# A streaming encoder layer: the convolution's gated input computed with tokens on partitions

## The chip, the cores and the metric

The kernel runs on one core of a Trainium2 chip. A core has five engines that run side by side, each with its own queue of instructions: TensorE (matrix products and transposes, PE in the profile, its weight loads PEld), VectorE (DVE), ScalarE (ACT), GpSimd (POOL) and SyncE (SP, which here issues most of the transfers between main memory and the core). TensorE writes to eight PSUM tiles of 128 x 512 fp32, which VectorE and ScalarE read. The metric is the device time of one execution in microseconds (us); less is better.

## What is computed

One inference step of one layer for 384 tokens: 256 of a new stream and 8 x 16 of running streams. Cut to what matters here:

```python
h = rmsnorm(x, norm_mix_g)                      # x: 384 x 2048
proj = h @ w_in                                 # columns: GLU in | q | k | v | forget | gate A | gate B
u = glu_in[..., :D_CONV] * sigmoid(glu_in[..., D_CONV:])      # D_CONV = 1024
ext = concatenate([conv_buf, u], axis=1)
z = layernorm(causal_dwconv(ext, conv_dw_w, conv_dw_b), ...)  # 31 taps
a_out = (z * sigmoid(z)) @ conv_pw_out
new_conv = ext[:, -(CONV_W - 1):]               # an output
q = rmsnorm(q, q_norm_g); k = rmsnorm(k, k_norm_g)            # 8 heads of 128
b_out = attn_fn(q, k, v, logf) @ w_att_out
x = x + (gate_a * a_out + gate_b * b_out) @ w_out
# then a gated feed-forward with a 3-tap convolution
```

Outputs are x, the new keys, values and forget logarithms, and the convolutions' new states, all in fp32.

## The kernel before

**Tiling.** 384 tokens are three blocks of 128. The normed input is kept transposed, features on partitions (`hT`, four tiles of four 128-feature blocks). To keep fp32 accuracy every operand of a large product is split into a high and a low part (`hi`, `lo`), and each product is three matmuls: high by high, high by low, low by high (L239 to L241, L244 to L246).

**Weights.** `plan` is the list of all weight tiles in order. `ahead` fetches the next ones (two or three in advance; three raw and three split buffers) and `split` makes the high part on ScalarE (L145) and the low part on VectorE (L146). A pair of 128-row blocks of weights is one fetch, one split, and then the matmuls.

**Jobs.** `gemm` runs a list of jobs, each a block of columns of a projection. A job of kind "B" puts tokens on the output partitions: three PSUM tiles, up to 512 columns. A job of kind "A" puts features there: four PSUM tiles of 384 tokens. PSUM has five tiles in `acc` and three in `misc`; a job takes `acc` tiles, side work takes `misc`. When the last product of a job is done its `evac` functions read the tiles. After each k step `tick` lets side work take one step; TensorE runs everything in the order in which the program emits it.

**Stages around the change.** First stage: value blocks 0 and 1 run together, while `x_chunk` turns the input into `hT`, two blocks at a time, on TensorE (transposes L285, high part L288 on ScalarE, low part L289 on VectorE), and `first_norm` sums squares and gets the row scale `rs1`. Then value block 2, keys, queries. Then the gated input in four jobs of kind "A", with two side works: attention, one head every six steps (`head_operands` turns that head's queries and keys with six TensorE transposes, L583 and L587; `head_scores`, `head_probs`, `head_out`, `head_last`), and the convolution: `conv` lets channel block c start `CONV_LAG` steps after block c-1; its taps are VectorE instructions (L720, L722), and `fill` copies the block's input and turns its last rows on TensorE (L708, L709) to write the state. Next the two gates, beside the rest of the convolution and its LayerNorm (`layer_norm`, its first product is L779), the output projections, and the feed-forward.

**Order.** On ScalarE, VectorE and GpSimd a planner orders instructions by priority and by its own estimate of time; `tc.high_priority(offset=...)` moves a block ahead (`SPLIT_AHEAD` for splits, `EVAC_AHEAD` for evacuations). `queued` chains an instruction behind the newest chained one of its engine, so that the chain runs in the order of the program text. Before, only SP's first transfers are chained.

**Turning on VectorE.** A VectorE transpose works on blocks of 32 x 32. `blocks` (L255) turns a panel of 512 features with 16 such instructions, by writing each 32-row band to its place:

```python
for b in range(4):
    for a in range(4):
        nc.vector.transpose(put(a, slice(32 * b, 32 * b + 32)), src[32 * a:32 * a + 32, b])
```

It is used before the change for the mixed output, the second norm and the feed-forward.

Of the kernel before, what the change touches and what calls it, by code (L numbers as in the profile page):

```python
# [15 lines left out]
P = 128  # L16
# [3 lines left out]
H = 8  # L20
# [9 lines left out]
CONV_FIRST, CONV_LAG = 24, 17  # L30
# [3 lines left out]
SPLIT_AHEAD, EVAC_AHEAD = 150, 400  # L34
# [6 lines left out]
def hybrid_step(  # L41
# [66 lines left out]
    make_identity(nc, ident[:])  # L108

    def newton_rsqrt(r, s, m):  # L110
        nc.scalar.activation(s, m, AF.Sqrt)
# [32 lines left out]
    def split_rows(hi, lo, raw, o, k):  # L144
        nc.scalar.copy(hi[:, k, :o], raw[:, k, :o])  # L145
        tt(lo[:, k, :o], raw[:, k, :o], f(hi[:, k, :o]), op=ALU.subtract)  # L146
# [44 lines left out]
    v_last = len(plan) - 16  # L191
    ready = []
# [28 lines left out]
    def gemm(jobs, sides=()):  # L221
        for js in jobs:
            js = js if isinstance(js, tuple) else (js,)
            for j in js:
                nb = 4 if j["kind"] == "A" else NTT
                j["ps"] = [(misc_tile if j is not js[0] and i == 2 else acc_tile)() for i in range(nb)]
            for j, k in [(j, k + i) for k in range(0, js[0]["nk"], 2) for j in js for i in range(2)]:
# [7 lines left out]
                for m in range(nb):  # L235
                    s = slice(m * P, (m + 1) * P)
                    if j["kind"] == "A":
                        o = ps[m][:, :NT]
                        mm(o, hi[:, kk, s], ah, start=st, stop=False)  # L239
                        mm(o, hi[:, kk, s], al, start=False, stop=False)  # L240
                        mm(o, lo[:, kk, s], ah, start=False, stop=sp)  # L241
                    else:
                        o = ps[m][:, :n]
                        mm(o, ah[:, s], hi[:, kk, :n], start=st, stop=False)  # L244
                        mm(o, ah[:, s], lo[:, kk, :n], start=False, stop=False)  # L245
                        mm(o, al[:, s], hi[:, kk, :n], start=False, stop=sp)  # L246
                if sp:
                    with tc.high_priority(offset=EVAC_AHEAD):
                        for m in range(nb):
                            j["evac"](m, ps[m])  # L250
                    if "done" in j:
# [3 lines left out]
    def blocks(rows, put):  # L255
        src = rows.rearrange("p t (m b j) -> p b m t j", m=4, b=4)
# [11 lines left out]
    def job(kind, nk, act, evac, n=512, done=None):  # L268
        d = dict(kind=kind, nk=nk, act=act, evac=evac, n=n)
# [12 lines left out]
    def x_chunk(c):  # L282
# [5 lines left out]
        nc.scalar.activation(hi, ps[:, :NT], AF.Identity, scale=g)  # L288
        stt(lo, ps[:, :NT], g, f(hi), op0=ALU.mult, op1=ALU.subtract)  # L289
# [34 lines left out]
    rs1b = cp.tile([P, NT], F32, name="rs1b")  # L324
# [22 lines left out]
    for v, r, n in rows:  # L347
        nc.gpsimd.dma_start(vrow[r:r + n, :], v[0].rearrange("(c p) -> c p", p=P))
    kg = p_qkv.tile([P, P], F32, name="kg")
    nc.gpsimd.dma_start(kg[:], k_norm_g[0].partition_broadcast(P))  # L350
    bf = p_qkv.tile([P, H], F32, name="bf")
    nc.gpsimd.dma_start(bf[:], b_forget[0].partition_broadcast(P))
# [35 lines left out]
    def first_norm():  # L388
        for c in range(2, 16, 2):
# [6 lines left out]
            if c % 4 == 2:  # L396
                for t in range(NTT):
                    n = c // 4
                    tc.keep_in_program_order(
                        nc.scalar.activation(junk[:], xs[n][:, t, :], AF.Square, accum_out=ssx[:, t, n:n + 1]))  # L400
            yield
            if c > 2:
                yield
        mt = p_x0.tile([P, NTT], F32, name="mt")
        nc.vector.tensor_reduce(mt[:], ssx[:], axis=mybir.AxisListType.X, op=ALU.add)
        ts(mt[:], mt[:], 1.0 / DM, EPS, op0=ALU.mult, op1=ALU.add)
        r = rsqrt(mt[:], [P, NTT], p_x0, "r1")
        nc.vector.tensor_copy(rs1[:], r[:])
        for _ in range(12):
            yield  # L410
        small_columns()
        yield
        dg = diagonals(p_x0.tile([P, NTT, P], F32, name="r1d"), rs1)
        yield
        yield
        over_partitions(dg, rs1b[:])
# [6 lines left out]
    def tok_evac(dst, c0, n, sq=None, shared=True):  # L423
        def ev(t, ps):
            if shared and t % 2:
                ts(dst[:, t, c0:c0 + n], ps[:, :n], rs1[:, t:t + 1], None, op0=ALU.mult)
            else:
                nc.scalar.activation(dst[:, t, c0:c0 + n], ps[:, :n], AF.Identity, scale=rs1[:, t:t + 1])
            if sq is not None:
                for i in range(n // P):  # L430
                    jk = p_qkv.tile([P, P], F32, tag="jk", bufs=2, name="jk")
                    h = c0 // P + i
                    nc.scalar.activation(jk[:], dst[:, t, h * P:(h + 1) * P], AF.Square,
                                         accum_out=ssq[:, sq, t, h:h + 1])
# [3 lines left out]
    v_jobs = [job("B", 16, ha, tok_evac(vt, 344 * i, 344, shared=i == 2), n=344) for i in range(3)]  # L438
    gemm([(v_jobs[0], v_jobs[1]), v_jobs[2]], [first_norm()])
    close_x0()  # L440
# [23 lines left out]

    nc.sync.dma_start(prompt_v[0, 0].rearrange("(t p) h d -> p t (h d)", p=P), vt[:, 0:2, 0:1024])
    nc.sync.dma_start(sample_v[0].rearrange("b t h d -> (b t) (h d)"), vt[:, 2, 0:1024])
# [47 lines left out]
    gemm([job("B", 16, ha, tok_evac(kt, 512 * i, 512, 0)) for i in range(2)], [bias_rows()])  # L514
    close_b()
    rk = head_rsqrt(0)
# [6 lines left out]

    gemm([job("B", 16, ha, tok_evac(qt, 512 * i, 512, 1)) for i in range(2)])
# [548 lines left out]
```

## Time and profile before

| | |
|---|---|
| median of 3 runs | 2005.61 us (2002.94 to 2005.78) |
| the profiled execution | 2005.83 us |
| its span, first to last instruction | 2003.9 us |
| granted TensorE clock, mean | 0.999 |
| matmul records | 9431 |
| bytes moved | 275.99 MB, mean 138 GB/s |
| first stage with value blocks (first product 7.21, keys from 85.74) | 78.5 us |
| keys and queries (85.74 to 218.46) | 132.7 us |
| gated input and attention (218.46 to 390.05) | 171.6 us |

In the profile a group's row names the line, the engine, the operation, the tiles it writes and reads and how often it ran; then its busy time, the mean of one in ns, and the idle time before it with what ended it. A row of the timeline gives the start, the duration, the engine and the instruction, and in brackets the wait just before it. A row of windows gives the stretch, its length, then busy time and count for PE, PEld, DVE, ACT and POOL, the granted clock, the share of time in which the transfer engines were busy, and GB/s. Matmuls overlap: their pace is read from starts.

### The profile page before, as it was taken

The page shows a single profiled execution, that of the slowest core. Times are in us where ns is not written, and L with a number is a line of the kernel's source. Part 1 is how long each engine was busy: PE and PEld are TensorE (multiplying, and loading weights), DVE is VectorE, ACT ScalarE, POOL GpSimd, SP SyncE. Part 2 cuts the span into 40 slices and gives each one's busy share as a digit, 9 for nine tenths or more (in the row PEclk, how much of TensorE's full clock was granted, in tenths as well). Part 3 has the DMA queues.
Part 4 walks back from the last instruction along what each step waited for, and adds up shares of the span by engine and source line. Part 5 has one row for each costly group of instructions (what it writes and reads, how often), then busy time and mean ns, then how long its engine had stood idle before and what let it go on. Part 6 is the DMA issues. An engine that isn't in the chain of part 4 may idle for free.

```text
span 2003.9 us, 24493 instructions
## 1 busy us (share of the span) xinstructions
PE 1992.6 (99%) x9431; PEld 1681.5 (84%) x9431; DVE 1272.2 (63%) x1852; ACT 742.1 (37%) x1077; POOL 87.2 (4%) x216
## 2 busy tenths in 40 slices
PE   8999999999999999999999999999999999999999
PEld 8988999988888887888888888888888888888887
DVE  4435478888765487676867683367673376638663
ACT  5434455433334523334433432233332233323321
POOL 2000001100000000000010000001000000000000
PEclk9999999999999999999999999999999999999999
DMA  6566566444444334534444444444443444344443
GB/s 179 176 175 175 137 163 167 120 140 131 132 134 125 127 121 142 185 121 133 127 137 116 137 127 137 126 127 126 129 135 127 133 120 137 126 129 125 137 157 106
DMA packets 209254, 275.99 MB, mean 138 GB/s; under 512 B 55878, under 2 KB 96729, under 8 KB 209129
## 3 DMA queue, kind: packets, MB, share of 16 engines
q1 hardware_dynamic: 208817, 273.85, 46.3%
q8 instruction: 74, 1.21, 0.2%
q0 software_dynamic: 288, 0.57, 0.2%
q14 instruction: 43, 0.35, 0.1%
q10 hardware_dynamic: 32, 0.01, 0.0%
HBM read 266.98 MB, written 7.86 MB: 137 GB/s over the span
## 4 chain that ended last, share of the span: by engine, by line
PE 95%; DVE 4%; issue 1%; DMA 1%; ACT 0%; SPq 0%; ACTq 0%; DVEq 0%
PE acc L244 28%; PE acc L246 28%; PE acc L245 28%; PE acc L239 2%; PE acc L241 2%; PE acc L240 2%; DVE mixT L259 1%; DVE lo L146 1%; DMA raw<-in_w_in_dram 1%; DVE sgA L843 0%; DVE uT L259 0%; DVE sgA L844 0%; PE misc L636 0%; PE misc L603 0%; PE misc L285 0%
## 5 line engine op out<-in xcount | busy, mean ns | idle before, releaser
L146 DVE TENSOR_TENSOR lo<-raw,hi 128x1024 fp32r<-128x1024 f32 (+2 forms) x481 | 579.6, 1205 | 582.7 <-ACT hi L145 579.0
L145 ACT CAST hi<-raw 128x1024 fp32r<-128x1024 f32 (+2 forms) x481 | 496.0, 1032 | 994.2 <-PE acc L246 869.1
L244 PE MATMUL acc<-hi,xg 128*128 128x512 f32 x1056 | 411.8, 390 | 0.0
L246 PE MATMUL acc<-hi,xg 128*128 128x512 f32 x1056 | 410.9, 389 | 0.0
L245 PE MATMUL acc<-lo,xg 128*128 128x512 f32 x1056 | 410.8, 389 | 0.0
L244 PE MATMUL acc<-hi,hT 128*128 128x512 f32 (+1 forms) x704 | 268.5, 381 | 2.4 <-ACT hT L288 2.4
L246 PE MATMUL acc<-hi,hT 128*128 128x512 f32 (+1 forms) x704 | 266.0, 378 | 0.4 <-DVE hT L289 0.4
L245 PE MATMUL acc<-lo,hT 128*128 128x512 f32 (+1 forms) x704 | 265.8, 377 | 0.0
L244 PEld LDWEIGHTS acc<-hi,xg 128*128 128x128 f32 x1056 | 198.2, 188 | 42.3
L246 PEld LDWEIGHTS acc<-hi,xg 128*128 128x128 f32 x1056 | 198.2, 188 | 41.3
L245 PEld LDWEIGHTS acc<-lo,xg 128*128 128x128 f32 x1056 | 198.2, 188 | 40.6
L244 PE MATMUL acc<-hi,act 128*128 128x512 f32 x528 | 205.5, 389 | 0.5 <-DVE y L1018 0.5
L246 PE MATMUL acc<-hi,act 128*128 128x512 f32 x528 | 205.4, 389 | 0.0
L245 PE MATMUL acc<-lo,act 128*128 128x512 f32 x528 | 205.4, 389 | 0.0
L722 DVE SCALAR_TENSOR_TENSOR ut<-ext,cw,ut 128x384 f32<-128x384 f32 x240 | 151.5, 631 | 6.1
L244 PEld LDWEIGHTS acc<-hi,hT 128*128 128x128 f32 x704 | 132.7, 189 | 25.3 <-ACT hT L288 2.7
L246 PEld LDWEIGHTS acc<-hi,hT 128*128 128x128 f32 x704 | 132.7, 189 | 23.3 <-DVE hT L289 0.7
L245 PEld LDWEIGHTS acc<-lo,hT 128*128 128x128 f32 x704 | 132.8, 189 | 22.2
L259 DVE STREAM_TRANSPOSE extf<-tok 32x384 f32<-32x384 f32 x176 | 100.3, 570 | 30.9 <-ACT tok L954 28.2
L259 DVE STREAM_TRANSPOSE uT<-tok 32x384 f32<-32x384 f32 x176 | 100.3, 570 | 29.7 <-ACT tok L954 26.9
L244 PEld LDWEIGHTS acc<-hi,act 128*128 128x128 f32 x528 | 99.1, 188 | 21.6 <-DVE y L1018 0.9
L245 PEld LDWEIGHTS acc<-lo,act 128*128 128x128 f32 x528 | 99.1, 188 | 20.5
(289 smaller groups left out, 2079.7 us busy)
## 6 DMA issues: line engine op xcount, KB each, us to landing
raw<-in_w_up_dram SPq DMA_DIRECT2D x176, 512.0 KB
raw<-in_w_in_dram SPq DMA_DIRECT2D x96, 512.0 KB
raw<-in_w_down_dram SPq DMA_DIRECT2D x88, 512.0 KB
raw<-in_w_in_dram SPq DMA_DIRECT2D x64, 256.0 KB
raw<-in_w_out_dram SPq DMA_DIRECT2D x32, 512.0 KB
raw<-in_w_att_out_dram SPq DMA_DIRECT2D x16, 512.0 KB
raw<-in_conv_pw_out_dram SPq DMA_DIRECT2D x16, 512.0 KB
raw<-in_w_in_dram SPq DMA_DIRECT2D x23, 344.0 KB
```

The source lines that it names most:

```text
L145: nc.scalar.copy(hi[:, k, :o], raw[:, k, :o])
L146: tt(lo[:, k, :o], raw[:, k, :o], f(hi[:, k, :o]), op=ALU.subtract)
L239: mm(o, hi[:, kk, s], ah, start=st, stop=False)
L240: mm(o, hi[:, kk, s], al, start=False, stop=False)
L241: mm(o, lo[:, kk, s], ah, start=False, stop=sp)
L244: mm(o, ah[:, s], hi[:, kk, :n], start=st, stop=False)
L245: mm(o, ah[:, s], lo[:, kk, :n], start=False, stop=False)
L246: mm(o, al[:, s], hi[:, kk, :n], start=False, stop=sp)
L259: nc.vector.transpose(put(a, slice(32 * b, 32 * b + 32)), src[32 * a:32 * a + 32, b])
L722: stt(o, v, wc, o, op0=ALU.mult, op1=ALU.add)
```

## The change

- The gated input's jobs become jobs like the others, tokens on partitions: three PSUM tiles of 512 columns (256 of the sigmoid half, 256 of the linear half). ScalarE takes the sigmoid straight from PSUM with the row scale, VectorE multiplies, and `blocks` turns each panel of 256 features into `ut`. The states are written from the unturned rows with two transfers, in place of TensorE transposes, ScalarE copies and 16 transfers. The turned row scale `rs1b` is gone.
- Queries and keys are turned on VectorE by `blocks`, panel by panel, in the stage after their own (into `attT` and into the queries' tile); `head_operands` has no TensorE work any more.
- Order of the projection: value blocks 0 and 2, queries, keys, value block 1, gated input. The value outputs are written after block 1. Sums of squares for queries and keys are taken after the evacuations (`post`).
- In the first stage casts, splits, input blocks, the last sums of squares, the square root, the scaled evacuations of the values, and GpSimd's identity and small transfers are chained by `queued`.
- `wide` jobs take their third PSUM tile from `misc`: all but the first stage, the last value block and the gated input.
- Attention's steps get a priority of their own, 250; cached values and bias rows are loaded in separate steps; the convolution starts at step 32 with a lag of 15 in place of 24 and 17.

```diff
-CONV_FIRST, CONV_LAG = 24, 17
+CONV_FIRST, CONV_LAG = 32, 15
-SPLIT_AHEAD, EVAC_AHEAD = 150, 400
+SPLIT_AHEAD, ATT_AHEAD, EVAC_AHEAD = 150, 250, 400
...
     def split_rows(hi, lo, raw, o, k):
-        nc.scalar.copy(hi[:, k, :o], raw[:, k, :o])
-        tt(lo[:, k, :o], raw[:, k, :o], f(hi[:, k, :o]), op=ALU.subtract)
+        first = in_first()
+        queued(nc.scalar.copy(hi[:, k, :o], raw[:, k, :o]), first)
+        queued(tt(lo[:, k, :o], raw[:, k, :o], f(hi[:, k, :o]), op=ALU.subtract), first)
...
-    planned(w_in, 0, V_COLS[0], 16, V_COLS[1])
-    for cols in V_COLS[2:] + K_COLS + Q_COLS + GLU_COLS + GA_COLS + GB_COLS:
+    planned(w_in, 0, V_COLS[0], 16, V_COLS[2])
+    for cols in Q_COLS + K_COLS + V_COLS[1:2] + GLU_COLS + GA_COLS + GB_COLS:
...
+    def in_first():
+        return len(plan) >= v_last - 4
...
-                nb = 4 if j["kind"] == "A" else NTT
-                j["ps"] = [(misc_tile if j is not js[0] and i == 2 else acc_tile)() for i in range(nb)]
+                j["ps"] = [(misc_tile if i == 2 and (wide or j is not js[0]) else acc_tile)() for i in range(NTT)]
...
         hi, lo = hT[c // 4][:, 0, c % 4, :], hT[c // 4][:, 1, c % 4, :]
-        nc.scalar.activation(hi, ps[:, :NT], AF.Identity, scale=g)
-        stt(lo, ps[:, :NT], g, f(hi), op0=ALU.mult, op1=ALU.subtract)
+        with tc.high_priority(offset=EVAC_AHEAD):
+            queued(nc.scalar.activation(hi, ps[:, :NT], AF.Identity, scale=g))
+            queued(stt(lo, ps[:, :NT], g, f(hi), op0=ALU.mult, op1=ALU.subtract))
...
+    def q_panel(n):
+        blocks(qt[:, :, 512 * n:512 * (n + 1)], by_feature(attT[:, 4 * n:4 * n + 4]))
+        for h in range(4 * n, 4 * n + 4):
+            nc.scalar.activation(attT[:, h], attT[:, h], AF.Identity, scale=qgs[:])
+
+    kT = qt[:].rearrange("p t n -> p (t n)").rearrange("p (h x) -> p h x", h=H)
+
+    def k_panel(n):
+        blocks(kt[:, :, 512 * n:512 * (n + 1)], by_feature(kT[:, 4 * n:4 * n + 4]))
+
+    for n in range(2):
+        after(2 + 10 * n, lambda n=n: q_panel(n))
+    gemm([tok_job(kt, 512 * i, 512, 0) for i in range(2)], wide=True)
...
+    for n in range(2):
+        after(3 + 10 * n, lambda n=n: k_panel(n))
+    gemm([v_jobs[1]])
...
     def glu_evac(g):
-        def ev(m, ps):
-            if m < 2:
-                sgb[m] = p_att.tile([P, NT], F32, tag="sgb", bufs=2, name="sgb")
-                tt(sgb[m][:], ps[:, :NT], rs1b[:], op=ALU.mult)
-                nc.scalar.activation(sgb[m][:], sgb[m][:], AF.Sigmoid)
-            else:
-                u = ut[:, 2 * g + m - 2, :]
-                tt(u, ps[:, :NT], rs1b[:], op=ALU.mult)
-                nc.gpsimd.tensor_tensor(u, u, sgb[m - 2][:], op=ALU.mult)
+        def ev(t, ps):
+            sgb = p_att.tile([P, 256], F32, tag="sgb", bufs=2, name="sgb")
+            nc.scalar.activation(sgb[:], ps[:, 0:256], AF.Sigmoid, scale=rs1[:, t:t + 1])
+            stt(ur[:, t, 256 * g:256 * (g + 1)], ps[:, 256:512], rs1[:, t:t + 1], sgb[:], op0=ALU.mult, op1=ALU.mult)
         return ev
+
+    def glu_done(g):
+        def done():
+            blocks(ur[:, :, 256 * g:256 * (g + 1)], by_feature(ut[:, 2 * g:2 * g + 2]))
+            if g == 3:
+                nc.sync.dma_start(sample_conv[0, :, 14:30, :], ur[:, 2, :])
+                nc.sync.dma_start(prompt_conv[0, 0], ur[98:128, 1, :])
+        return done
...
-            tr(ps[:, :P], ut[:, c, 2 * P:], ident[:])
-            tr(ps[:32, P:2 * P], ut[:, c, 224:256], ident[:])
...
-    gemm([job("A", 16, ha, glu_evac(g)) for g in range(4)], [att_steps, conv_steps])
+    gemm([job(16, ha, glu_evac(g), done=glu_done(g)) for g in range(4)], [att_steps, conv_steps])
```

More of the change, by code (lines that the diff above doesn't have):

```diff
@@ L427, in ev @@
             else:
[L428 to L434, printed above, removed]
+                queued(nc.scalar.activation(dst[:, t, c0:c0 + n], ps[:, :n], AF.Identity, scale=rs1[:, t:t + 1]),
+                       in_first())
         return ev
     ha = grouped(hT)
-    v_jobs = [job("B", 16, ha, tok_evac(vt, 344 * i, 344, shared=i == 2), n=344) for i in range(3)]
-    gemm([(v_jobs[0], v_jobs[1]), v_jobs[2]], [first_norm()])
-    close_x0()
+    v_jobs = [job(16, ha, tok_evac(vt, 344 * i, 344, shared=i == 2), n=344) for i in range(3)]
+    norm_steps = first_norm()
+    gemm([(v_jobs[0], v_jobs[2])], [norm_steps])
     def tiny(name):
@@ L1022, in evac @@
             return ev
-        return [job("B", 4 * len(gs), grouped(tiles), evac(n)) for n in range(4)]
+        return [job(4 * len(gs), grouped(tiles), evac(n)) for n in range(4)]
     for what, g in FFN_PLAN:
-        gemm(up_jobs(g) if what == "up" else down_jobs(g, g[-1] == 10))
+        gemm(up_jobs(g) if what == "up" else down_jobs(g, g[-1] == 10), wide=True)
     pe_order.__exit__(None, None, None)
```

168 lines of the change are left out of this document (84 added, 84 removed).

## The prediction

> **What bounds the kernel now.** First the page: the busy line of TensorE and the chain that ended last.
>
> ```profile
> span 2003.9 us, 24493 instructions
> PE 1992.6 (99%) x9431; PEld 1681.5 (84%) x9431; DVE 1272.2 (63%) x1852; ACT 742.1 (37%) x1077; POOL 87.2 (4%) x216
> ...
> PE 95%; DVE 4%; issue 1%; DMA 1%; ACT 0%; SPq 0%; ACTq 0%; DVEq 0%
> ```
>
> TensorE is busy or pipelined for 99% of the span, and the chain runs through it for 95%. Next the view of waits for TensorE alone, where a gap worth filling would stand:
>
> ```profile
> PE misc L308 <- POOL ident masks.py:199: 2.5, 1, 2.5
> PE acc L244 <- ACT hT L288: 2.4, 1, 2.4
> PE acc L244 <- DVE y L1018: 0.5, 1, 0.5
> ```
>
> Three rows make nearly all its waiting (total, times, longest), the two large ones in the first 20 us. So an edit gains only by taking instructions off TensorE's own queue or by closing the gap in the first stage; work moved to another engine is free until that engine makes TensorE wait. I go through the change in that order.
>
> **The gated input's matmuls.** Before, each of the four jobs runs 16 x 4 x 3 matmuls of 384 columns, 768 in all; after, 16 x 3 x 3 of 512 columns, 576 in all. The product is the same; the pace of one decides. The timeline of TensorE gives it by starts, since durations overlap:
>
> ```profile
> 385.02 0.33 PE L240 MATMUL acc<-hT,hi 128*128 128x384 f32 x1
> ...
> 389.87 0.33 PE L241 MATMUL acc<-hT,lo 128*128 128x384 f32 x1
> ...
> 609.80 0.39 PE L244 MATMUL acc<-hi,hT 128*128 128x512 f32 x1
> ...
> 617.28 0.39 PE L244 MATMUL acc<-hi,hT 128*128 128x512 f32 x1
> ```
>
> From 385.02 to 389.87 lie 28 steps: 0.1732 us each. From 609.80 to 617.28 lie 33 steps: 0.2267 us each. 768 x 0.1732 = 133.0 and 576 x 0.2267 = 130.6, so **-2.4 us**; the swap of operands by itself is worth little.
>
> **Turns taken off TensorE.** Per head six transposes (L583, L587); per channel block two (L708, L709); once three products in two passes for the row scale (L334, six records).
>
> ```profile
> 235.13 0.49 PE L583 MATMUL misc<-ident,qt 128*128 128x128 f32 x3
> 235.45 0.49 PE L587 MATMUL misc<-ident,kt 128*128 128x128 f32 x3
> 235.70 0.42 PE L239 MATMUL acc<-hT,hi 128*128 128x384 f32 x1
> 235.96 0.33 PE L240 MATMUL acc<-hT,hi 128*128 128x384 f32 x1
> ...
> 548.32 0.27 PE L708 MATMUL misc<-ident,ut 128*128 128x128 f32 x1
> 548.45 0.48 PE L244 MATMUL acc<-hi,hT 128*128 128x512 f32 x1
> 548.77 0.40 PE L245 MATMUL acc<-lo,hT 128*128 128x512 f32 x1
> ...
> 79.39 0.83 PE L334 MATMUL misc<-r1d,ones 128*128 128x128 f32 x6
> 79.98 0.40 PE L244 MATMUL acc<-hi,hT 128*128 128x344 f32 x1
> 80.22 0.32 PE L245 MATMUL acc<-lo,hT 128*128 128x344 f32 x1
> ```
>
> One head: 235.70 - 235.13 = 0.57 us, and the first matmul after it takes 0.26 to the next start in place of 0.17: 0.09 more. 8 x 0.66 = **-5.3**. One channel block: 0.13 + (0.32 - 0.23) = 0.22; 8 of them **-1.8**. The row scale: 0.59 + about 0.08 = **-0.7**. These lie wholly on the bounding queue and nothing can hide them, so nothing of them can be lost except as a new wait.
>
> **The first stage.** The queue of transfers keeps its order; what the chain changes is the order on ScalarE and VectorE, which becomes that of the program text: cast 3, block 2, block 3, cast 4. Now it is this:
>
> ```profile
> 11.56 0.49 PE L285 MATMUL misc<-ident,xs 128*128 128x128 f32 x3
> 12.85 0.77 ACT L145 CAST hi<-raw 128x688 fp32r<-128x688 f32 x1 [3.96 <-DMA raw<-in_w_in_dram]
> 13.65 0.87 DVE L146 TENSOR_TENSOR lo<-raw,hi 128x688 fp32r<-128x688 f32 x1 [3.76 <-ACT hi L145]
> 14.94 0.77 ACT L145 CAST hi<-raw 128x688 fp32r<-128x688 f32 x1 [1.32 <-DMA raw<-in_w_in_dram]
> 15.61 0.57 ACT L288 ACTIVATE hT<-misc,gm 128x384 fp32r<-128x384 f32 x1
> ...
> 17.19 0.45 PE L246 MATMUL acc<-hi,hT 128*128 128x344 f32 x1 [0.38 <-DVE hT L289]
> ...
> 7.20:13.78 6.58, 6.58 (x44) 6.32 (x42) 2.34 (x5) 2.46 (x4) 2.89 (x10) 1.00 0.98 259
> ...
> 17.45:20.86 3.41, 3.41 (x13) 3.41 (x13) 1.00 (x2) 1.93 (x6) 0.00 (x0) 0.50 0.89 265
> ```
>
> The activation block for L288 had long left TensorE (its transposes start at 11.56), but ScalarE stood 1.32 us before a cast whose weights had not landed. With the block ahead of that cast, its high half runs 13.62 to 14.20, its low half after the split, 14.52 to 15.13, so the matmul that now starts at 17.19 starts at about 15.1: **-2.1**. More can't be had from the order, because the cast at 12.85 waits for a transfer in a stretch where the transfer engines are busy 0.98 of the time. The identity, too, is ready earlier (the 2.5 us row above), but everything after it ends at the same transfer: 0. The last row shows 3.41 us at a granted clock of 0.50 behind the gap, worth 1.7 us more if it vanishes; I leave it in. Bounds for this part: -4.2 (order, L289's 0.4, clock) and +1.3 (a chained cast that waits as long as the 1.32 above with a ready block behind it).
>
> The Trainium skill ("TensorE: Matmul & The Clock Gate", The HAM clock gate) says that the clock falls after an idle window of about 3.4 us, free-running. Here a wait of 2.44 us was followed by a halved stretch, so the trace disagrees on the length; a remaining gap of 1.3 us could still be charged. If the page's reading held for the shorter gap, the estimate by it would be 1.7 us lower.
>
> **New waits at the ends of jobs.** Before, one VectorE read frees a PSUM tile; after, ScalarE's sigmoid and then VectorE's product must both have read it. These jobs hold three of five tiles, so the next job's third tile waits for the first tile's readers: it is covered by 12 matmuls x 0.2267 = 2.7 us. The readers cost as follows:
>
> ```profile
> L146 DVE TENSOR_TENSOR lo<-raw,hi 128x1024 fp32r<-128x1024 f32 x32 | 39.3, 1235 | 11.2 <-ACT hi L145 10.1 <-DMA sc<-in_state_conv_dram 1.0
> L674 DVE TENSOR_TENSOR sgb<-acc,rs1b 128x384 f32<-128x384 f32 x8 | 4.2, 552 | 0.2 <-PE acc L241 0.2
> L675 ACT ACT_TABLE_LOAD x4 | 5.1, 1283 | 2.7 <-DVE sgb L674 2.7
> L145 ACT CAST hi<-raw 128x1024 fp32r<-128x1024 f32 x32 | 33.3, 1047 | 51.3 <-PE acc L240 44.9 <-DMA raw<-in_w_in_dram 6.3
> ```
>
> Table load 1.28, then 256 columns on each engine at about 0.45 (two thirds of the 0.55 for 384, plus start-up): 2.2 us, hidden; with a cast (1.05) and a low half (1.24) in the way, 4.5 us, 1.8 over. Three joints: 0 to +5.4; I take 0.3 each, **+0.9**, nearer the covered end since evacuations are planned ahead of the splits. PSUM tiles borrowed from the second pool in the other stages: 0, at best -1.1 (the small rows of the wait view, with those below its first four).
>
> **VectorE.** This is what hides all the turning, so its room is counted.
>
> ```profile
> 62.60:85.70 23.10, 23.10 (x150) 23.09 (x149) 8.51 (x13) 8.98 (x14) 0.00 (x0) 1.00 0.60 162
> ...
> 218.40:390.00 171.60, 171.60 (x1239) 165.16 (x1239) 133.83 (x294) 84.79 (x177) 16.04 (x23) 1.00 0.60 149
> 390.00:588.00 198.00, 198.00 (x879) 163.57 (x878) 163.01 (x229) 72.57 (x99) 10.16 (x17) 1.00 0.47 135
> 588.00:618.00 30.00, 30.00 (x134) 24.81 (x134) 9.38 (x8) 8.53 (x9) 0.00 (x0) 1.00 0.45 133
> ...
> L722 DVE SCALAR_TENSOR_TENSOR ut<-ext,cw,ut 128x384 f32<-128x384 f32 x79 | 50.6, 641 | 1.6
> L519 DVE TENSOR_TENSOR kt<-kt,rq0r 128x1024 f32<-128x1024 f32 x3 | 3.6, 1220 | 0.0
> ...
> L259 DVE STREAM_TRANSPOSE uT<-tok 32x384 f32<-32x384 f32 x176 | 100.3, 570 | 29.7 <-ACT tok L954 26.9
> L699 DVE STREAM_TRANSPOSE ext<-sc 128x256 f32<-128x256 f32 x4 | 1.7, 437 | 0.0
> ```
>
> Queries: 32 turns x 0.57 = 18.2 us in the key stage, where VectorE is mostly free. Keys: two multiplies by three at 1.22 (7.3), 32 turns (18.2), eight low halves of 0.87 (7.0): 32.5 us beside the last value block, whose matmuls take about 22.8 (the first row's stage), so some 10 us spill into the gated-input stage; the first scores there come nine steps, some 20 us, in. Gated input: 64 turns of 192 elements, about 0.38 by the two rows (0.437 at 256, 0.570 at 384, one ns an element), 24.2 us, and 12 products of 0.45, 5.4. Gone are about 8 for L674 and L678, 4.4 key copies, 4.4 of queries. Net 22 us on 133.8 in a stage that shrinks from 171.6 to about 164: 95% against 78%. Convolution taps can give way; they are needed at the LayerNorm's product at 618. Until there VectorE is idle for 37.8 + 35.0 + 20.6 = 93 us; less 22, less 9 of shorter stages, less 12 for LayerNorm six steps earlier, 50 us remain. So 0 on the path. Transfers: both value outputs (two issues) move behind the last value block and so past the queries', keys' and bias transfers on SP's queue; 16 small state writes become two; bias rows go ahead of values. The DMA share is 0.60 in the row above and no matmul there waits for a landing, so 0; without that cover a weight tile would come late, as at 12.85, by about an us.
>
> **Sum:** -2.4 - 5.3 - 1.8 - 0.7 - 2.1 + 0.9 = -11.4. The profiled execution took 2005.83 us (span 2003.88 and 1.95 around it), 0.2 over the median 2005.61 of the runs shown. Forecast 2005.8 - 11.4 = **1994.4 us**.
>
> **Rivals.**
> (a) More: the clock is not halved (-1.7), evacuations are covered (-0.9), joints of the other stages close (-1.1): 1990.7. For it: each gap is seen. Against: the first transfer still comes at 12.85.
> (b) Little: the order gains nothing in front, and all three joints cost 1.8: -10.2 + 5.4, so 2001.0. For it: the table load of 1.28 stands before the sigmoid. Against: evacuations stand 400 ahead in priority, splits 150.
> (c) Slower: VectorE becomes the bound beside the gated input. If its 37.8 us of idle time there are waits that stay, 156 + 38 = 194 us stand against 164: 30 late. If one channel's 31 taps (0.64 each, 20 us) give way, 10 are left, 2004.4; if none, 2024.4; the middle, **2014**. It decides against the change once low halves L146 come over 11.4 us late in all. For it: 95% of a stage in fixed order. Against: splits keep their priority over turns and taps, and 50 us are spare. The Trainium skill ("VectorE: DVE Perf Modes", Rules for kernel authors) advises TensorE for 128 x 128 turns and VectorE for 32 x 32; by that rule (c) is the outcome. The trace disagrees on this kernel's balance, with TensorE at 99%.
> (d) The conversion doesn't bring matmuls of 512 columns to 0.2267 beside attention: at 0.232, 3 us less gain, 1997.4, inside the forecast's own range. For it: attention's small products break the stream in that stage, not at 609. Against: they break it today as well.
>
> **Chances.** A run-to-run difference under 0.2% (4 us) can't be told from no change, so 2001.6 is the line. Forecast 0.50 (own range 1991 to 1999, (d) in it), (a) 0.12, (b) 0.22, (c) 0.16. Faster: 0.50 + 0.12 + 0.14 of (b) = 0.76; same: 0.08 of (b) and 0.02 of (c) = 0.10; slower 0.14. The range of 8 in 10 reaches from (a)'s 1988 to 2007, the low end of (c); what is left out is most of (c) and a tail below.
>
> **What would show it.** No rows for L583, L587, L708 and the first L334; in the gated-input stage starts 0.227 apart and a stage of about 164 us before the gates; a first-stage gap under 1.5 us that ends near 15; TensorE's wait view without rows for VectorE's low half, the keys' turns or the sum before LayerNorm. A row of several us for any of these would make (c) or (b) right; a wait on sigmoid or product at three joints would price (b).

## The result and the profile after

| | before | after |
|---|---|---|
| median | 2005.69 us (4 runs, 2002.94 to 2005.85) | 2031.09 us (4 runs, 2030.54 to 2032.64) |
| span of the profiled execution | 2003.9 us | 2030.6 us |
| granted clock, mean | 0.999 | 0.991 |

The ratio is 1.013, interval 1.0118 to 1.0143: the kernel became slower by 25 us where 11 us of gain were forecast, and 2031.09 lies above the range. The page of after, its first lines and the chain that ended last:

```profile
span 2030.6 us, 24013 instructions
PE 1987.0 (98%) x9169; PEld 1650.2 (81%) x9169; DVE 1315.2 (65%) x1965; ACT 743.9 (37%) x1065; POOL 81.3 (4%) x208
...
PE 89%; DVE 8%; issue 1%; DMA 1%; SPq 1%; ACT 0%; POOL 0%; DVEq 0%; ACTq 0%
```

TensorE has 262 matmul records fewer, as meant, but the chain now runs through VectorE for 8%, against 4% before (a share that by itself says little: in the mended kernel below it is 10%). Starts of TensorE's stages, read off the timelines, say where the time went (the last two columns belong to experiments below):

| start, us | before | after | pool_k_unprio | no_chain |
|---|---|---|---|---|
| first product | 7.21 | 6.23 | 6.23 | 6.24 |
| last matmul of the first two value blocks | 62.08 | 58.89 | 58.77 | 61.50 |
| gated input | 218.46 | 214.23 | 214.11 | 220.46 |
| first output projection | 655.17 | 684.01 | 645.73 | 651.76 |
| end of the span | 2003.9 | 2030.6 | 1992.3 | 1998.3 |

After is 4.2 us ahead when the gated input starts and 28.8 us behind when the gates end. TensorE's waits (total, times, longest) show two events there, in one row:

```profile
PE misc L648 <- DVE mx L625: 35.3, 2, 26.9
```

L648 is the first matmul of `head_out`. It needs one of three `misc` tiles, and all three hold the scores of the next head until VectorE's L625 has added the bias rows `bs` and reduced them. So a late L625 stops TensorE's queue. The timeline around the first wait, SP's issues included:

```profile
239.16 0.47 SPq L584 DMA_DIRECT2D bs<-c_dr  x1
239.79 4.05 SPq L574 DMA_DIRECT2D kc<-in_cache_k_dram  x4
244.10 1.06 SPq L139 DMA_DIRECT2D raw<-in_w_in_dram  x2
253.21 2.24 SPq L574 DMA_DIRECT2D kc<-in_cache_k_dram  x4
255.55 1.12 SPq L139 DMA_DIRECT2D raw<-in_w_in_dram  x2
268.51 2.32 SPq L574 DMA_DIRECT2D kc<-in_cache_k_dram  x4
270.93 3.19 SPq L139 DMA_DIRECT2D raw<-in_w_in_dram  x6
274.17 0.47 SPq L585 DMA_DIRECT2D bs<-c_dr  x1
...
275.26 1.04 ACT L148 CAST hi<-raw 128x1024 fp32r<-128x1024 f32 x1 [10.18 <-DMA raw<-in_w_in_dram]
278.33 1.15 POOL L590 TENSOR_TENSOR bs<-bs,mk 128x256 f32<-128x256 f32 x1 [119.28 <-DMA bs<-c_dr]
279.51 0.29 DVE L625 CUSTOM_DVE_ANT_0 pr<-misc,bs 128x128 f32<-128x128 f32 x1 [0.61 <-POOL bs L590]
279.87 0.80 PE L648 MATMUL misc<-vt,pT 128*128 128x128 f32 x2 [8.39 <-DVE mx L625]
```

The four parts of one head's bias rows (L584 to L587) are issued 35 us apart: the first at 239.16, the second at 274.17. Between them on SP's queue, which issues in order, stand three heads' keys (12 issues) and five weight tiles (two issues each). The keys' issues themselves stood still for a buffer, from 256.67 (255.55 + 1.12) to 268.51; the weights behind them were late too, for ScalarE waited 10.18 us. SP's own waits give that a row:

```profile
SPq L574 <- DVE qz L606: 20.4, 3, 11.9
```

Before the change the same head's four parts were issued one behind the other, with the keys after them, and SP's waits there have no row for the keys:

```profile
243.51 0.41 SPq L557 DMA_DIRECT2D bs<-c_dr  x1
...
244.91 0.61 SPq L560 DMA_DIRECT2D bs<-d_dr  x1
245.62 0.40 SPq L550 DMA_DIRECT2D kc<-in_cache_k_dram  x1
```

The second wait, same view of after:

```profile
331.95 0.39 PE L245 MATMUL acc<-hi,hT 128*128 128x512 f32 x1
...
335.85 15.18 DVE L737 SCALAR_TENSOR_TENSOR ut<-ext,cw,ut 128x384 f32<-128x384 f32 x22
...
340.94 0.76 POOL L591 TENSOR_TENSOR bs<-bs,mk 128x128 f32<-128x128 f32 x1
...
353.10 5.91 DVE L737 SCALAR_TENSOR_TENSOR ut<-ext,cw,ut 128x384 f32<-128x384 f32 x11
358.92 0.29 DVE L625 CUSTOM_DVE_ANT_0 pr<-misc,bs 128x128 f32<-128x128 f32 x1
359.27 0.80 PE L648 MATMUL misc<-vt,pT 128*128 128x128 f32 x2 [26.93 <-DVE mx L625]
```

Here the bias rows were complete at 341.70 (340.94 + 0.76), yet VectorE came to L625 at 358.92: more than thirty convolution taps, from 335.85 on, stand ahead of it in VectorE's fixed order. So the wait from 332.34 on has two parts: 9.4 us in which the rows themselves were late, and 17.5 us of VectorE's order. The rows were late on SP's queue again, this time behind weights:

```profile
322.25 0.35 SPq L584 DMA_DIRECT2D bs<-c_dr  x1
332.85 0.89 SPq L139 DMA_DIRECT2D raw<-in_w_in_dram  x2
333.79 3.21 SPq L585 DMA_DIRECT2D bs<-c_dr  x1
```

From 322.60 to 332.85 SP issued nothing; its longest wait for a weight buffer that VectorE's low half (L149) has to free is 10.2 us (10.6 before the change, where the four parts of a head went together). And both waits were followed by a halved clock, by the windows view:

```profile
275.90:286.10 10.20, 6.23 (x32) 4.92 (x33) 5.34 (x17) 5.25 (x14) 1.66 (x4) 0.50 0.77 207
337.30:364.70 27.40, 5.43 (x30) 4.31 (x31) 25.90 (x55) 4.03 (x13) 4.44 (x7) 0.50 0.46 122
```

TensorE's 6.23 and 5.43 us of work at half pace cost 3.1 and 2.7 us. Waits and clock together are 35.3 + 5.8 = 41.1 us, and 2031.1 - 41.1 = 1990.0: without the two events the kernel would be a little below the forecast; the best variant below gets 38.3 of these 41.1 us back by the spans (2030.6 - 1992.3). So the questions are what makes the events, and whether the gain is there without them.

### The profile page after: what moved, and what is told of

It reads as the page before. It is cut to its first block, busy times and chain, and to the rows that moved or that the text cites. A ratio compares the mean times of both kernels' runs of the same rounds, so it can differ in the third digit from the quotient of the medians.

```text
span 2030.6 us, 24013 instructions
## 1 busy us (share of the span) xinstructions
PE 1987.0 (98%) x9169; PEld 1650.2 (81%) x9169; DVE 1315.2 (65%) x1965; ACT 743.9 (37%) x1065; POOL 81.3 (4%) x208
## 4 chain that ended last, share of the span: by engine, by line
PE 89%; DVE 8%; issue 1%; DMA 1%; SPq 1%; ACT 0%; POOL 0%; DVEq 0%; ACTq 0%
PE acc L243 20%; PE acc L244 20%; PE acc L245 20%; PE misc L244 9%; PE misc L245 9%; PE misc L243 9%; DVE ut L737 4%; DVE lo L149 2%; DMA raw<-in_w_in_dram 1%; DVE ut L260 0%; DVE mixT L260 0%; SPq L139 0%; PE misc L652 0%; PE misc L286 0%; DVE sgA L861 0%
## 5 line engine op out<-in xcount | busy, mean ns | idle before, releaser
L149 DVE TENSOR_TENSOR lo<-raw,hi 128x1024 fp32r<-128x1024 f32 (+2 forms) x481 | 580.2, 1207 | 568.4 <-ACT hi L148 564.2
L243 PE MATMUL acc<-hi,xg 128*128 128x512 f32 x704 | 274.9, 390 | 0.0
L245 PE MATMUL acc<-hi,xg 128*128 128x512 f32 x704 | 273.9, 389 | 0.0
L244 PE MATMUL acc<-lo,xg 128*128 128x512 f32 x704 | 273.9, 389 | 0.0
L243 PEld LDWEIGHTS acc<-hi,xg 128*128 128x128 f32 x704 | 132.1, 188 | 28.4
L245 PEld LDWEIGHTS acc<-hi,xg 128*128 128x128 f32 x704 | 132.1, 188 | 27.4
L244 PEld LDWEIGHTS acc<-lo,xg 128*128 128x128 f32 x704 | 132.2, 188 | 27.1
L737 DVE SCALAR_TENSOR_TENSOR ut<-ext,cw,ut 128x384 f32<-128x384 f32 x240 | 141.3, 629 | 1.9
L245 PE MATMUL misc<-hi,xg 128*128 128x512 f32 x352 | 137.0, 389 | 0.0
L243 PE MATMUL misc<-hi,xg 128*128 128x512 f32 x352 | 137.0, 389 | 0.0
L244 PE MATMUL misc<-lo,xg 128*128 128x512 f32 x352 | 136.9, 389 | 0.0
L243 PE MATMUL acc<-hi,act 128*128 128x512 f32 x352 | 136.9, 389 | 0.0
L244 PE MATMUL acc<-lo,act 128*128 128x512 f32 x352 | 136.9, 389 | 0.0
L245 PE MATMUL acc<-hi,act 128*128 128x512 f32 x352 | 136.9, 389 | 0.0
```

Of the source, the lines that this page charges most:

```text
L149: queued(tt(lo[:, k, :o], raw[:, k, :o], f(hi[:, k, :o]), op=ALU.subtract), first)
L737: stt(o, v, wc, o, op0=ALU.mult, op1=ALU.add)
```

## Experiments

Theory Q: SP's queue carries the bias rows too late. Theory V, the prediction's rival (c): VectorE has too much to do. Theory C: the convolution's taps, now later and denser, crowd out the scores. Where one execution alone was timed, the text says so; the kernel before took 2004.1 to 2005.6 us (median) beside them.

**loads_ahead**: bias rows and values get the same priority as attention's steps.

```diff
-                if step is head_probs and d["h"] + 2 < H:
-                    load_b(d["h"] + 2)
-                if step is head_probs and 0 < d["h"] < H - 1:
-                    load_v(d["h"] + 1)
+                with tc.high_priority(offset=ATT_AHEAD):
+                    if step is head_probs and d["h"] + 2 < H:
+                        load_b(d["h"] + 2)
+                    if step is head_probs and 0 < d["h"] < H - 1:
+                        load_v(d["h"] + 1)
```

> The changed kernel, with the bias rows' and cached values' loads of attention put under the same priority (250) as attention's steps. Theory Q (queue): those loads have no priority while the steps that read them, the keys' loads (250) and the weights (150) have one, so SP issues them last; two scores wait for late bias rows, and a third of a channel's taps and more are ordered before them. It expects both waits of TensorE (8.4 and 26.9 us, with about 6 us of halved clock behind them) gone: 2031.1 - 35.3 - 6 = 1990, 1985 to 1997. Theory V (VectorE has too little room once the gated input, queries and keys are turned there) expects at most a shift of the waits: over 2015. Theory C (the convolution's taps, later and denser at 32 and 15, crowd out the scores) expects the same as V: over 2015.

Measured: 2018.84 us, ratio 1.0069 (1.0054 to 1.0084). Both score waits are gone, and others stand in their place; TensorE's two largest:

```profile
PE acc L243 <- ACT hi L148: 15.7, 3, 6.4
PE acc L244 <- DVE lo L149: 5.1, 5, 3.1
```

and on SP's queue:

```profile
SPq L579 <- PE misc L652: 18.3, 6, 11.3
SPq L584 <- DVE mx L625: 13.5, 2, 7.3
```

Now values (L579) and bias rows (L584) stand at the head of SP's queue until their buffers are free, and the weights queue behind. Bias rows in time remove L648's wait, as Q says; that this alone is enough is refuted. The time lies where V and C had put it, but these waits are for weights and not for score reductions.

**no_att_prio**: attention's steps without their priority of 250.

```diff
-                with tc.high_priority(offset=ATT_AHEAD):
-                    step(d)
+                step(d)
```

> The changed kernel without the priority of attention's steps, so that steps, keys' loads, bias rows and values stand in program order again, as before the change. Theory Q: the bias rows come in time, both waits go: 1990, 1985 to 1998. Theory V: scores fall behind turns and taps even more often: over 2025. Theory C: over 2015.

Measured: 2012.36 us, ratio 1.0038 (1.0024 to 1.0053). The first wait is gone, a second of 17.4 us stays at L648. There the bias rows are complete at 325.7 and VectorE reaches the scores at 338.83, behind some 18 taps more and one turn of keys: lateness on SP is not the whole cause. No theory had this time in its range.

**no_turn**: the turns' load taken from VectorE, the program's order kept; the convolution reads a constant, so the outputs are not the layer's.

```diff
+    nc.gpsimd.memset(ut[:], 0.5)
...
-            blocks(ur[:, :, 256 * g:256 * (g + 1)], by_feature(ut[:, 2 * g:2 * g + 2]))
```

> The changed kernel without the 64 VectorE turns of the gated input; the convolution reads a constant in its place (the output is not the reference's). VectorE is 24 us lighter in that stage. Theory V: the waits go or nearly so, 1985 to 1997. Theory Q: the bias rows keep their place in SP's queue, so a wait of 8 us or more stays before the third head's scores and one of over 15 us later: over 2010. Theory C: taps start earlier but stay as dense: over 2005.

Measured: 2028.16 us (one run). TensorE's wait is nearly as long as in after:

```profile
PE misc L648 <- DVE mx L625: 34.0, 2, 25.6
```

The turns are what the change puts on VectorE in this stage, 24 us of them by the prediction's estimate; without them 1.3 us of 35.3 go, and the same 22 and 11 taps stand before the reduction. V falls for this wait: it names VectorE, but not for the load that the change adds.

**conv_24_17**: the convolution's start and lag as before the change.

```diff
-CONV_FIRST, CONV_LAG = 32, 15
+CONV_FIRST, CONV_LAG = 24, 17
```

> The changed kernel with the convolution's start and lag set back to 24 and 17 steps. Theory C: the waits go, 1985 to 1997. Theory Q: the loads keep their place behind keys and weights, so at least one wait over 8 us stays: over 2000, up to 2035. Theory V: the room is the same, so 2010 to 2035.

Measured: 2017.66 us (one run). One score wait of 19.7 us and one of 2.6 remain. The taps' place matters, but putting it back doesn't cure it.

**pool_loads**: bias rows and values issued on GpSimd's queue.

```diff
-        nc.sync.dma_start(vc[:], cache_v[0, :, :, h, :].rearrange("b p d -> p b d"))
+        nc.gpsimd.dma_start(vc[:], cache_v[0, :, :, h, :].rearrange("b p d -> p b d"))
...
-        nc.sync.dma_start(bs[:, 0:P], c_dr[h, 0:P].partition_broadcast(P))
+        nc.gpsimd.dma_start(bs[:, 0:P], c_dr[h, 0:P].partition_broadcast(P))
...
```

> The changed kernel with attention's bias rows and cached values loaded through GpSimd's queue in place of SP's; priorities stay. Theory Q, now narrower: SP's queue is in order, and what is lost is that loads of attention and weights hold each other up there; with two of the three kinds of load elsewhere, scores and weights both come in time: 1990, 1985 to 2000. Theory S: the cached keys are now turned only three steps before the scores that use them (four before), and it is this late chain that the taps get in front of, whatever the bias rows do: a wait of over 8 us before some scores stays, over 2002.

Measured: 1997.92 us, ratio 0.9965 (0.9952 to 0.9978). What TensorE still waits for in this stage:

```profile
PE acc L243 <- ACT hi L148: 2.9, 1, 2.9
PE acc L244 <- DVE lo L149: 1.7, 3, 0.8
```

With these loads off SP's queue nothing is left of L648's 35 us, and the change is a gain. That also speaks against the expectation's theory S, by which a wait over 8 us would have stayed. The 2.9 us are a late weight tile: keys still stand ahead of weights on SP.

**prio_conv_back**: no priority, and 24 and 17 (the edits of no_att_prio and conv_24_17).

> The changed kernel without the priority of attention's steps and with the convolution's start and lag at 24 and 17; steps and loads of attention stay at their new places. Theory D (each of the two helps by itself by 13 to 19 us, together they leave nothing): no wait before scores, 1988 to 1998. Theory S: the late chain of cached keys stays, so a wait stays: 2000 to 2015.

Measured: 2003.37 us (one run), with one score wait of 9.3 us. These two settings together still leave a score wait, where theory D expected none.

**sched_before**: the change's computation in the order of before: offsets of attention's steps, no priority, loads at their old places, 24 and 17.

```diff
-            for off, step in ((1, head_operands), (4, head_scores), (9, head_probs),
-                              (12, head_out), (14, head_last)):
+            for off, step in ((0, head_past_keys), (2, head_operands), (4, head_scores), (9, head_probs),
+                              (11, head_out), (13, head_last)):
...
-                with tc.high_priority(offset=ATT_AHEAD):
-                    step(d)
-                if step is head_probs and d["h"] + 2 < H:
+                step(d)
+                if step is head_out and d["h"] + 2 < H:
+                    load_v(d["h"] + 2)
...
```

> The changed kernel with everything about the order of attention and convolution as before the change: no priority, the steps' old places, values and bias rows loaded together two heads ahead, start and lag 24 and 17. The turning on VectorE, the gated input's new form, the first stage and the order of the projection stay as changed. Theories Q, S and D: no wait of TensorE over 3 us in that stage, so what is left are the gains: 1990, 1986 to 1996. Theory V, for the third time: the new form itself needs more VectorE than there is, 2005 or more.

Measured: 2005.63 us over 10 runs, ratio 1.0001 (0.9992 to 1.0011). The time lies in V's range (2005 or more), and here the turns do stand in the way. The forecast gain is spent on waits again, small ones, with 13.7 us at half clock behind them:

```profile
PE misc L647 <- DVE mx L624: 5.3, 2, 2.9
PE misc L663 <- DVE on L653: 2.1, 1, 2.1
PE misc L614 <- DVE pz L641: 1.6, 1, 1.6
```

and VectorE's timeline shows why the old order doesn't serve:

```profile
252.30 6.11 DVE L260 STREAM_TRANSPOSE ut<-ur 32x192 f32<-32x192 f32 x16
...
305.51 2.68 DVE L260 STREAM_TRANSPOSE ut<-ur 32x192 f32<-32x192 f32 x7
308.22 0.29 DVE L624 CUSTOM_DVE_ANT_0 pr<-misc,bs 128x128 f32<-128x128 f32 x1
```

Sixteen turns run as one block of 6.1 us ahead of attention's small instructions, and the last seven of another sixteen stand right before a score reduction for which TensorE waits from 306.16 to 308.58. That is order once more and not a lack of time, as pool_k_unprio below shows with the same turns. It suggests that the change needs a priority for attention, with the same care for its loads; no run takes that priority alone out of a kernel whose loads are in time.

**sched_before_conv_new**: sched_before with the convolution at 32 and 15.

> The one before, but with the convolution's new start and lag, 32 and 15. Theory Q: the same as the one before within 4 us, 1986 to 1998. Theory D: the denser taps alone bring a wait back, 1998 to 2012.

Measured: 2020.11 us (one run), the longest wait 19.2 us at the score reduction. The 14 us between this and sched_before come from the taps' start and lag alone, the only edit between the two.

Two theories were left for the second wait. K: the keys' load, which sits inside the priority and so goes ahead, is the sole cause. P: the taps are placed ahead of the scores on VectorE, whatever the queue does.

**k_unprio**: keys issued outside the priority; all loads on SP.

```diff
-        if d["h"] + 1 < H:
-            load_k(d["h"] + 1)
...
+                if step is head_operands and d["h"] + 1 < H:
+                    load_k(d["h"] + 1)
```

> The changed kernel with one thing moved: the load of the next head's cached keys is issued after attention's step and outside its priority; the step itself keeps it. Theory K (the cause is this load: lifted 250 ahead with the step, it stands in SP's queue before weights and bias rows, and waits there for VectorE to be done with the old keys): the bias rows come in time and both waits go, 1990, 1986 to 1998. Theory Q without K (any load of attention on SP's queue does it): a wait of 5 us or more stays, 2000 to 2020.

Measured: 2017.34 us, ratio 1.0066 (1.005 to 1.0081). The first wait is gone; the other, in the timeline:

```profile
320.82 0.39 PE L245 MATMUL acc<-hi,hT 128*128 128x512 f32 x1
321.69 0.45 POOL L591 TENSOR_TENSOR bs<-bs,mk 128x128 f32<-128x128 f32 x1
323.51 14.76 DVE L737 SCALAR_TENSOR_TENSOR ut<-ext,cw,ut 128x384 f32<-128x384 f32 x22
...
339.35 3.19 DVE L737 SCALAR_TENSOR_TENSOR ut<-ext,cw,ut 128x384 f32<-128x384 f32 x5
342.46 0.28 DVE L623 CUSTOM_DVE_ANT_0 pr<-misc,bs 128x128 f32<-128x128 f32 x1
342.81 0.79 PE L646 MATMUL misc<-vt,pT 128*128 128x128 f32 x2 [21.60 <-DVE mx L623]
```

The bias rows are complete at 322.14, and 27 taps still stand before the reduction at 342.46. K as the sole cause falls: the first wait is the keys', the second is the order on VectorE.

**pool_k_unprio**: pool_loads and k_unprio together.

> Bias rows and values on GpSimd's queue and the keys' load outside the priority. Of the variant with GpSimd's queue alone one wait of 2.9 us for weights and three of 1.7 us in all are left, behind keys on SP's queue. Both theories: these go, 1990 to 1995 (1997.9 without them and a halved stretch of 3.4 us).

Measured: 1993.62 us, ratio 0.9946 (0.9929 to 0.9962): faster than before by 10.5 us against 2004.1 on its chip, and the best of those timed in several runs. Its window over the stretch where after waited 27 us:

```profile
337.30:364.70 27.40, 27.40 (x176) 22.32 (x175) 26.47 (x64) 15.40 (x29) 2.29 (x4) 1.00 0.49 132
```

VectorE is busy for 26.47 of 27.40 us there and TensorE doesn't wait for it at all. The taps are the same; they stand elsewhere, in the timeline of the same kernel:

```profile
329.62 0.77 POOL L591 TENSOR_TENSOR bs<-bs,mk 128x128 f32<-128x128 f32 x1
...
332.58 1.92 DVE L737 SCALAR_TENSOR_TENSOR ut<-ext,cw,ut 128x384 f32<-128x384 f32 x3
334.42 0.28 DVE L623 CUSTOM_DVE_ANT_0 pr<-misc,bs 128x128 f32<-128x128 f32 x1
```

Taps go in groups of one to four between attention's instructions. So moving the loads changed VectorE's order too. That fits a planner that puts taps first where it expects bias rows late; no run shows its estimates, so this link is argued and not shown.

**pool_b**: only the bias rows on GpSimd's queue.

> The changed kernel with the bias rows alone on GpSimd's queue; values and keys as changed. Theory K and Q: it is the bias rows that were late, so no wait of TensorE before scores is left; values (L579) still stand behind keys, weights may wait: 1994 to 2006. If values count as much as bias rows: over 2008.

Measured: 2008.15 us (one run). No score wait; TensorE waits 8.4 us for the cached values instead, and 3.7 us for weights. Every kind of load on the shared queue has to be in time.

**pool_k_conv**: pool_k_unprio with 24 and 17.

> The variant with GpSimd's queue and the keys' load outside the priority, and the convolution's start and lag at 24 and 17. Theory D (denser taps cost by themselves): 2 us or more under the same with 32 and 15. Theories K and Q: with the loads in time the lag no longer matters, within 3 us of it.

Measured: 1993.34 us (one run). With the loads in time the convolution's lag is worth nothing; the 13 us of conv_24_17 were its effect on an order that was already broken.

**scores_first**: after, with every tap ordered on VectorE behind the newest score reduction emitted before it; the loads stay as they are.

```diff
-                stt(o, v, wc, o, op0=ALU.mult, op1=ALU.add)
+                after_scores(stt(o, v, wc, o, op0=ALU.mult, op1=ALU.add))
```

> The changed kernel with one order added on VectorE: a tap emitted after a head's score reductions comes behind them; all loads stay as changed. Theory P (planner's order): the bias rows are late in fact by only part of the waits, the rest is VectorE doing taps that the planner put before scores whose bias rows had landed. Of the 26.9 us wait the rows account for 332.3 to 341.7, 9.4 us, so 17 us go; the first wait of 8.4 us stays: 2031 - 17 = 2014, with less halved clock down to 2005. Theory L (the late landing is the whole of it): 2025 or more.

Measured: 2008.29 us (one run):

```profile
PE misc L656 <- DVE mx L632: 12.0, 2, 8.7
```

The wait of 8.4 us, where the rows themselves are late, stays at 8.7; that of 26.9 falls to 3.3 (12.0 - 8.7). So the taps ahead of the scores made most of the second wait, as P says, and the two events have different causes. The 3.3 us that stay end with the bias rows (GpSimd's L590 ends at 334.35, the reduction starts at 334.38); why the rows were less late than in after is not shown.

**k_unprio_scores_first**: both order edits, all loads on SP.

> The variant with the keys' load outside the priority (one wait of 21.6 us left) and the same order of taps behind scores. There the sixth head's bias rows were ready at 322.2, 1.4 us into the wait. Theory P: the wait shrinks below 5 us: 2017.3 - 17 - 3 = 1997, 1990 to 2002. Theory L: 2010 or more.

Measured: 2000.93 us (one run). The score wait is 1.7 us; keys are now late, 6.4 us in two waits, with 6.8 us at half clock behind the longer.

**before_pool**: the control, the kernel before with its bias rows and values on GpSimd's queue.

> The kernel before with the values' and bias rows' loads on GpSimd's queue, nothing else. It is the control for the 1993.6 us of the changed kernel with its loads moved: TensorE waits for nothing in that stage before the change, so no gain, 2003 to 2007. If the moved loads themselves are worth the 10 us, 1997 or less.

Measured: 2005.17 us over 10 runs, ratio 0.9999 (0.999 to 1.0009). The moved loads are worth nothing by themselves, so the gain of pool_k_unprio is the change's.

**no_chain**: pool_k_unprio without the chain of the first stage (casts, splits, input blocks, squares, value evacuations) and without the priority of the input blocks that came with it.

```diff
-        return len(plan) >= v_last - 4
+        return False
...
-        with tc.high_priority(offset=EVAC_AHEAD):
-            queued(nc.scalar.activation(hi, ps[:, :NT], AF.Identity, scale=g))
...
+        nc.scalar.activation(hi, ps[:, :NT], AF.Identity, scale=g)
...
```

> The variant at 1993.6 us without the chain of casts, splits, input blocks, squares and evacuations in the first stage (GpSimd's chain and the order of the projection stay). By the forecast's step the chain is worth 2.1 us, with the halved clock up to 4.2: 1995.7 to 1997.8. If the chain does nothing: 1993.6.

Measured: 1999.50 us over 9 runs, ratio 0.9971 (0.9961 to 0.9981), 5.9 us over pool_k_unprio (6.0 by the spans) and above the expected range. About 1 us of that is the other chip (before: 2005.23 there, 2004.1 here), and the nine runs spread from 1996.78 to 2002.28, so the chain with its priority is worth about 5 us. New among TensorE's waits:

```profile
PE acc L243 <- ACT hT L289: 1.9, 2, 1.2
PE acc L243 <- DVE vt L435: 1.8, 1, 1.8
```

In the profiled execution, one of the slower of the nine, it is 2.7 us by the end of the first two blocks and 6.3 by the start of the gated input (last two columns of the table): the second row is the evacuation of the values at the joint, a place for which the prediction had no term.

## Why the prediction was wrong

**The step that failed** is the pair of noughts at the end of its costing: of VectorE "50 us remain. So 0 on the path", and of the transfers "The DMA share is 0.60 in the row above and no matmul there waits for a landing, so 0". It listed what moves on SP's queue, and then asked how busy the transfer engines were; and it counted VectorE's idle time. Neither figure tells of order. The transfers were not too many: in after they were stuck, in order, behind keys that a priority had lifted and that waited for a buffer (the first wait), and behind weights that waited for theirs (the second). VectorE had the time: pool_k_unprio does all the turning, and the longest wait of TensorE in that stage is 0.7 us. What cost 41 us is who stands before whom: on SP's queue (8.4 us, and 9.4 of the second wait), on VectorE (the other 17.5 us), and the clock behind each wait (5.8 us). Ordering the taps behind the scores took 23.6 us of the second wait away; why the planner had put them first stays open. The change gave attention's steps a priority of 250 with the keys' load inside and the bias rows' load outside it; the prediction passed over that.

**Rival (c)** had the sign by another mechanism. Its place, VectorE beside the gated input, is what the wait view names; no_turn, which removes the load and keeps the wait, speaks against it; in sched_before the turns do delay scores, by 2.4 us in the clearest case, but by their place. By the same runs the rule of the Trainium skill that the prediction weighed there ("VectorE: DVE Perf Modes", Rules for kernel authors: 128 x 128 turns to TensorE) did not decide here: with the order mended, turning on VectorE goes with 1993.62 us against 2004.1.

**The gain**, read from pool_k_unprio, whose loads alone differ from after, was 11.6 us by the spans (2003.9 - 1992.3) and 10.5 by the medians on its chip, against 11.4 forecast, but partly by errors that cancel:

- First stage to the start of the gated input: -4.35 (218.46 to 214.11) against -2.8 (chain and row scale). The chain was forecast at 2.1 with a bound of 4.2; taken away alone it is worth about 5, since it also prevents the joint wait and the halved clock that no_chain shows. No halved stretch stands behind the first gap any more, as rival (a) had it.
- Gated input and gates: 436.7 us before (218.46 to 655.17), 431.6 after the mend (214.11 to 645.73), -5.1 against -8.6. The conversion came as forecast: at the two paces, 768 x 0.1732 + 1152 x 0.2267 became 1728 x 0.2267, -2.4. The small products, by the starts, fell from 36.6 to 31.2 us, -5.4 against -5.6 (8 x 0.57 + 8 x 0.13). What failed is the rest: the sum over all starts of what large matmuls take above those paces rose from 5.9 to 8.6 us, +2.7, where the forecast had -0.6 (+0.9 for the joints, -1.5 for the broken pace beside the turns). About 1.0 stands at one joint of the gated input and 2.3 in single late steps of the gates, for which there was no term. -2.4 - 5.4 + 2.7 = -5.1. Rival (d)'s even slower pace didn't come; the steps away from interruptions are 0.227.
- From there to the end: -2.1 (1348.7 to 1346.6) against 0, at best -1.1. The output projections' and feed-forward's joints gave that; which part is due to `wide` was not tried alone.

**Left open**: by which estimates the planner places taps before scores; and the runs with one execution carry their verdicts by their waits, tens of us or a clear row, not by a time to a fraction of a per cent.

## What to carry to other kernels

When work leaves the bounding engine, list for each wait that this engine could meet what stands before the releasing instruction on every in-order queue; busy shares and idle sums don't show that. A step that is given priority needs all its loads in time as well, on a queue where they can't be held up by a load that is waiting for its buffer; here five issues a head on another queue turned 1.3% slower into 0.35% faster (0.54% with the keys out of the priority). And the engine that a wait names isn't shown to be overloaded until its load has been taken away and the wait has gone with it.

## What was not expected of the hardware

The halved clock comes after far shorter waits than the Trainium skill ("TensorE: Matmul & The Clock Gate", Part 1: The HAM clock gate) leads one to expect: the page has the clock fall after an idle window of about 3.4 us. In no_chain two gaps of 1.20 and 1.79 us (14.47 to 15.67, with 0.38 more just after it, and 61.82 to 63.61) are each followed by 3.41 us at 0.50:

```profile
16.73:20.14 3.41, 3.41 (x12) 3.41 (x13) 1.16 (x2) 2.08 (x7) 0.00 (x0) 0.50 0.86 263
64.52:67.93 3.41, 3.41 (x10) 2.62 (x9) 1.69 (x10) 2.11 (x4) 0.00 (x0) 0.50 0.54 154
```

The length agrees with the page: inside the kernels every halved stretch is a multiple of 3.41 us (10.24 and 27.31 in after), as fits its window that runs on regardless of the program. Not every short gap is charged: 1.66 and 2.68 us in k_unprio_scores_first were not. Nor is it always one window: in sched_before a wait of 2.42 us (306.16 to 308.58) goes with 6.83 us at half clock from 308.33 on:

```profile
308.33:315.16 6.83, 6.58 (x32) 5.19 (x33) 5.18 (x20) 2.41 (x8) 0.00 (x0) 0.50 0.37 107
```

So a wait of one to three us may cost up to about 3.4 us beyond itself, and one of 27 us cost 2.7.
